# Hybrid decoder layer: weight-sum transfers re-placed, and the token operand of the sums made by ScalarE

## The chip, the cores and the metric

One core of a Trainium2 chip runs one launch of the whole layer. The metric is the time of that launch on the device in microseconds (us). TensorE is called PE, VectorE DVE, ScalarE ACT, GpSimd POOL and SyncE SP, as the profile names them.

## The reference

The layer works on 512 tokens of width 1024 in float32.

```python
h = x + 0.5 * swiglu(rmsnorm(x, norm_ffn1), ffn1_gate, ffn1_up, ffn1_down)      # d_ff = 2816
u = rmsnorm(h, norm_mix)
... = split(u @ w_in)            # q, k, v of two attentions, gates, merge gates ga and gb
o_a = nsa(...)                   # compressed + selected + window attention, 8 heads of 64
o_b = banded_attention(...)      # window 128, learned sinks, 8 heads of 64
merged = sigmoid(ga) * (o_a @ w_branch_a) + sigmoid(gb) * (o_b @ w_branch_b)
h = h + merged @ w_out
h = h + 0.5 * swiglu(rmsnorm(h, norm_ffn2), ffn2_gate, ffn2_up, ffn2_down)
out = rmsnorm(h, norm_final)
```

Only the last lines are touched: the merge, the product with w_out, and the second FFN (ffn2).

## The kernel before, in words

Every operand of a matmul is kept as two parts, a rounded high part and the rest (`split`, line 389: ACT copies the high part, DVE subtracts it). A product takes three matmuls: high by high, high by low, low by high. Activations lie with features on the partitions: `h`, `uh` and `ul` are 8 blocks of 128 features by 512 tokens.

**Weights.** `Weights` (line 67) streams the weights as blocks of 128 x 1024. SP loads a raw block (line 143), ACT writes the high part `whi` (line 151), DVE the low part `wlo` (line 155). The ring has four slots. `next()` hands out block p and first prepares block p + 2 (`AHEAD`), whose raw load went out earlier (four raw buffers). So the ACT and DVE work for block p + 2 stands in those engines' queues right in front of whatever the code emits after `next()` for block p. Each engine runs its instructions in the order in which the code emits them (`manual_schedule`, line 372), and waits on semaphores alone.

**Seven products for eight.** Four of the 22 column tiles of ffn2's gate and up (`FOURS`, line 34: 0, 8, 12 and 17, each 512 columns wide in effect) and two of its three down stages (`down`, line 1971) are done with seven block products in place of eight. This needs sums of weight quarters and sums of token quarters.

- The weight sums are made in DRAM by DMA alone. `four_steps` (line 414) gives eight transfers for a group, `down_sums` (line 403) eight for a down stage: copies from one DRAM tensor to another, or accumulating transfers. `issue` (line 397) puts them on POOL's queue (lines 399 and 401). A step that reads what an earlier one wrote waits for its landing. Three generators hand them out one at a time: `in_mixers` (line 421) for the groups of tiles 0 and 8 and the first down stage, during attention; `in_merge` (line 428) for the group of tile 12; `in_ffn2` (line 434) for the second down stage and then the group of tile 17, sixteen steps.
- The token sums are made by `sums_of_tokens` (line 1723) for `four_hi` and `four_lo`. A call with even f makes the first half for feature block k = f // 2: the token operand of the blocks k and 4 + k (line 1731: `uh + ul` on DVE), two differences (lines 1733, 1734) and their split. A call with odd f makes the second half (lines 1738, 1739, then 1740) from what the first left.

**The merge gates** (from line 1754). For each of eight blocks d: loads of stored gate pre-activations (`load_z`, line 1747, with a POOL product with the norm's rows, line 1750), a load of `h` (line 1755), for every other d a gate product, the two branch products with sigmoids, and the split of the merged block. At the end of each d one step of `in_merge` (line 1774). POOL therefore meets the steps between its products of line 1750.

**The w_out loop** (from line 1777). For each d: the product, the addition to `h` (line 1780), then `norm_in` (line 658): ACT makes `uh = h * gain` (line 661), DVE `ul` (line 662), ACT the square (line 672), POOL the running sum `sqacc` (line 673). From d = 4 on one call of `sums_of_tokens` follows.

**ffn2** (from line 2093). `TILES` (line 35) sets the order 4, 5, group 0, 6, 7, first down stage; group 8, group 12, 16, second down stage; group 17, 21, the rest. Amid tile 4's products the norm is made: column sums of `sqacc` by PE (`norm_col`, line 675), a power on POOL (line 686), a few small DVE operations, rows `r_b` by PE and ACT (`norm_rows`, line 695). Tiles 4 and 5 each end with the transposes of four blocks of `h` into `o_t` (`residual`, line 2009). In tile 5, `make_room` (line 1792) gives the room of `h` to `left`, the store of the down stage's operands; `gated` (line 1816) makes the gated product, and after each odd tile `operands` (line 1836) writes that store. Then come two calls of `sums_of_tokens` and one `next(steps)` (`steps` is `in_ffn2()`). `four` (line 1849) is a group: seven products of two blocks each, with `next(steps)` after two of them (line 1886); `down` calls `next(steps)` at four of its fourteen blocks (line 1983).

Of the kernel before, what the change touches and what calls it, by code (L numbers as in the profile page):

```python
# [11 lines left out]
AF = mybir.ActivationFunctionType  # L12
OP = mybir.AluOpType
# [49 lines left out]
def f32(ap):  # L63
    return ap.bitcast(F32)


class Weights:
# [112 lines left out]
    def next(self):  # L180
        i = self.pos
        self.prep(i + self.AHEAD)
        self.pos += 1
        return self.place(i)
# [178 lines left out]
def layer(ctx, tc, a, out):  # L363
# [641 lines left out]
    with ExitStack() as mixing:  # L1005
# [717 lines left out]
        def sums_of_tokens(f, p0, names):  # L1723


            k, second = f // 2, f % 2
            tt, stt = vector.tensor_tensor, vector.scalar_tensor_tensor
            if not second:
                x, y = tokens["a"] = [p0.tile([128, S], F32, name=names[0]) for _ in range(2)]
                for o, d in ((x, k), (y, 4 + k)):  # L1730
                    tt(o, f32(uh[:, d]), f32(ul[:, d]), op=OP.add)
                p = tokens["p"] = p0.tile([128, 2, 256], F32, name=names[1])
                tt(p[:, 0], y[:, 256:], x[:, 256:], op=OP.subtract)
                tt(p[:, 1], x[:, :256], x[:, 256:], op=OP.subtract)
            else:
                (x, y), s1 = tokens["a"], tokens["p"][:, 0]
                p = p0.tile([128, 2, 256], F32, name=names[1])
                stt(p[:, 0], s1, -1.0, x[:, :256], op0=OP.mult, op1=OP.subtract)
                stt(p[:, 1], y[:, :256], -1.0, p[:, 0], op0=OP.mult, op1=OP.subtract)
            split(four_hi[:, k, 2 * second:2 * second + 2], four_lo[:, k, 2 * second:2 * second + 2], p)  # L1740
# [3 lines left out]
        with pool("merge", 2, side="right") as mp:  # L1744
            mh, ml = (mp.tile([128, KD, S], F32R, name=n, bufs=1) for n in ("mh", "ml"))

            def load_z(d):
                z = mp.tile([128, S], F32, name="z%d" % (d // KD))
                nc.sync.dma_start(z, zd[d])
                gpsimd.tensor_tensor(z, z, r_b, op=OP.mult)  # L1750
                return z

            za, zb = load_z(0), None
            for d in range(KD):
                nc.sync.dma_start(h[:, d], hd[d])
                gates_z = [za, zb]
                if d + 1 < KD:
                    za = load_z(d + 1)
                if d not in GB_EARLY:
                    gates_z[1] = mp.tile([128, S], F32, name="z1")  # L1760
                    ps = acc(False)
                    mm3(ps, W.next(), u_in, KD)
                    vector.tensor_tensor(gates_z[1], ps, r_b, op=OP.mult)
                if d + 1 in GB_EARLY:
                    zb = load_z(KD + d + 1)
                for z, x in zip(gates_z[::-1], (b_in, a_in)):
                    scalar.activation(z, z, AF.Sigmoid)
                    ps = acc(False)
                    mm3(ps.rearrange("p (t c) -> p t c", t=4), W.next(), x, 4)
                    vector.tensor_tensor(z, z, ps, op=OP.mult)  # L1770
                y, z = gates_z
                vector.tensor_tensor(y, y, z, op=OP.add)
                split(mh[:, d], ml[:, d], y)
                next(merge_steps, None)

            m_in = (lambda k: mh[:, k]), (lambda k: ml[:, k])
            for d in range(KD):
                ps = acc(False)
                mm3(ps, W.next(), m_in, KD)
                vector.tensor_tensor(h[:, d], ps, h[:, d], op=OP.add)  # L1780
                norm_in(d, 2)
                if d > 3:
                    sums_of_tokens(d - 4, mp, ("z0", "z1"))


    with pool("temp3", 2) as temp, pool("end") as end:
# [184 lines left out]
        def down():  # L1971


            home = {1: "acc", 6: "acc", 7: "acc", 5: "o", 3: "o", 2: "s", 4: "s"}
            gets = {1: ((0, 0, 0.5),), 5: ((0, 1, 0.5), (1, 1, 0.5)), 2: ((0, 0, 0.5),), 6: (), 3: ((0, 1, -0.5),),
                    4: ((1, 0, 0.5),), 7: ()}
            more = {6: ((0, 1, OP.subtract),), 7: ((1, 0, OP.add), (1, 1, OP.subtract))}
            banks = {}
            u = [temp.tile([128, 512], F32, name="y") for _ in range(2)]
            for n, (m, g) in enumerate(STEPS):  # L1980
                if n == 0:
                    turn_back()
                if n % 3 == 2:
                    next(steps, None)
                if g == 0:
                    banks[m] = [psum.tile([128, 512], F32, name=home[m]) for _ in range(2)]
                wh, wl = (w.rearrange("p (a b) c -> p a (b c)", a=2) for w in W.next())
                for t in range(2):
                    ps, c = banks[m][t], slice(t * 128, t * 128 + 128)
                    for q in range(2):  # L1990
                        ah, al = (x[:, 2 * g + q, LEFT[m], c] for x in (left_hi, left["lo"]))
                        mm(ps, ah, wh[:, q], g == q == 0, False)
                        mm(ps, al, wh[:, q], False, False)
                        mm(ps, ah, wl[:, q], False, g == q == 1)
                    if g == 0:
                        continue
                    if m == 1:
                        scalar.activation(u[t], ps, AF.Identity, scale=0.5)
                    if m in more:
                        vector.scalar_tensor_tensor(u[t], ps, 0.5, u[t], op0=OP.mult, op1=OP.add)  # L2000
                    for i, k, by in gets[m]:
                        y = o_t[:, 2 * i + t, k * 512:k * 512 + 512]
                        vector.scalar_tensor_tensor(y, ps, by, y, op0=OP.mult, op1=OP.add)
                    for i, k, op in more.get(m, ()):
                        y = o_t[:, 2 * i + t, k * 512:k * 512 + 512]
                        vector.tensor_tensor(y, y, u[t], op=op)
            turn[0] = 0

        def residual(d):

            ps = tbank()
            for t in range(4):
                tensor.transpose(ps[:, t], h[:, d, t * 128:(t + 1) * 128], ident)
            scalar.copy(o_t[:, :, d * 128:(d + 1) * 128], ps)
# [78 lines left out]
        for third, tiles in enumerate(TILES):  # L2093
            if third == 2:
                make_room_again()
            for n, f in enumerate(tiles):
                if f in FOURS:
                    four(f - THIRDS[third][0], third < 2)
                    next(steps, None)
                    turn[0] = 2  # L2100
                    continue
                first = third == n == 0
                gate_at, up_at = {}, {}
                if n > 1 or third:
                    gate_at = {2: turn_back, 6: turn_back}
                    up_at = {2: turn_back, 6: lambda: back(3 - third)}
                z = []
                if third < 2:
                    up_at[4] = lambda: z.append(scaled(pg))
                pg = acc(False)  # L2110
                wp = W.next()
                settle(later)
                mm3(pg, wp, u_in, KD, col if first else gate_at)
                if third == 2:
                    back(2)
                    next(last)
                pu = acc(False)
                mm3(pu, W.next(), u_in, KD, rows if first else up_at)
                if third == 0 and n < 2:
                    for d in range(4 * n, 4 * n + 4):  # L2120
                        residual(d)
                if third == 0 and n == 1:
                    make_room()
                if third < 2 and n + 1 == len(tiles):
                    W.prep(W.pos + 2)
                if not z:
                    z.append(scaled(pg))
                gated(z[0], pu, f - THIRDS[min(third, 2) if f != 16 else 2][0], third == 0)
                if third == 0 and n < 2:
                    for i in (4 + 2 * n, 5 + 2 * n):  # L2130
                        sums_of_tokens(i, temp, ("y", "t"))
                if not first:
                    next(steps, None)
            if third < 2:
                down()
        for _ in last:
# [26 lines left out]
```

## Time and profile before

| | us |
|---|---|
| median of 3 runs | 1144.85 |
| lowest and highest | 1142.98 and 1148.29 |
| the profiled execution, its own time | 1142.28 |
| its span in the profile | 1140.5 |

Times in the profile are counted from the start of the span. In a row of the order of time, the first number is the start and the second the duration; the brackets hold the idle time of the engine before it and what ended that. `x2` marks rows that were merged. A row with SPq, or a DMA row of POOL, is the issue of a transfer, not the transfer. In a row that groups issues, the last number is the median from issue to landing. In the chain of waits a row is start, length and what the chain stood on. The gates run from about 632 to 714 us, the w_out loop to about 755, tiles 4 and 5 to about 792, the group of tile 0 to about 841, and the first down stage starts near 872.

### The profile page before, as it was taken

What the parts mean: (1) busy time and instruction counts of PE and PEld (TensorE: products, weight loads), DVE (VectorE), ACT (ScalarE), POOL (GpSimd) and SP (SyncE); (2) the same over time, 40 slices, a digit from 0 to 9 for tenths busy, and PEclk for the clock granted to TensorE, in tenths of its full rate; (3) what the DMA queues carried; (4) which work ended last, traced back from release to release, by engine and by line L of the source; (5) the groups of instructions that cost most, each with busy time, mean ns of one, the idle gap of its engine ahead of it and who ended that gap; (6) DMA issues with size and microseconds to landing.
All of it is one profiled execution on the core that took longest, in us unless ns stands there. A gap on an engine that the chain in (4) does not pass through costs nothing.

```text
span 1140.5 us, 15817 instructions
## 1 busy us (share of the span) xinstructions
PE 1095.8 (96%) x5827; PEld 937.1 (82%) x5827; DVE 767.1 (67%) x1366; ACT 536.5 (47%) x980; POOL 218.8 (19%) x253
## 2 busy tenths in 40 slices
PE   9999999999999998999999998979769999999987
PEld 7888899988888998998888886867657888888876
DVE  5656787844555588987777356575637876787663
ACT  5433344532334466767667333434324545454432
POOL 0312120000003145834345323111110000000002
PEclk9999999999999999999999999989889999999999
DMA  6988988787756265359997899619998555645611
GB/s 209 265 230 197 253 184 254 227 280 252 257 176 176 75 185 181 116 155 275 262 272 216 231 229 305 179 56 257 267 268 239 185 184 166 203 141 192 208 69 74
DMA packets 201413, 232.43 MB, mean 204 GB/s; under 512 B 7924, under 2 KB 152120, under 8 KB 201016
## 3 DMA queue, kind: packets, MB, share of 16 engines
q1 hardware_dynamic: 172696, 159.98, 44.2%
q0 software_dynamic: 26176, 67.11, 25.4%
q10 hardware_dynamic: 2464, 4.33, 1.0%
q8 instruction: 46, 0.75, 0.3%
q14 instruction: 31, 0.25, 0.1%
HBM read 211.47 MB, written 87.03 MB: 262 GB/s over the span
## 4 chain that ended last, share of the span: by engine, by line
PE 81%; DVE 8%; DMA 4%; ACT 3%; issue 2%; POOL 0%; SPq 0%; POOLq 0%; ACTq 0%; DVEq 0%
PE acc L387 25%; PE o L387 18%; PE s L387 17%; PE s L1880 4%; PE o L1880 3%; PE acc L1880 3%; PE o L791 3%; DMA raw<-in_ffn_gate_dram 3%; PE tp L1647 2%; PE s L791 2%; PE acc L791 2%; DVE wlo L155 2%; DMA z<-zd 1%; ACT whi L151 1%; PE tp L387 1%
## 5 line engine op out<-in xcount | busy, mean ns | idle before, releaser
L155 DVE TENSOR_TENSOR wlo<-raw,whi 128x1024 fp32r<-128x1024 f32 (+2 forms) x225 | 260.9, 1180 | 87.8 <-ACT whi L151 86.0
L151 ACT CAST whi<-raw 128x1024 fp32r<-128x1024 f32 (+2 forms) x250 | 228.8, 938 | 136.0 <-PE acc L387 24.7
L387 PE MATMUL acc<-uh,whi 128*128 128x512 f32 x224 | 91.9, 410 | 8.7 <-ACT whi L151 8.7
L387 PE MATMUL acc<-uh,wlo 128*128 128x512 f32 x224 | 88.9, 397 | 0.0
L387 PE MATMUL acc<-ul,whi 128*128 128x512 f32 x224 | 88.6, 395 | 0.0
L387 PE MATMUL acc<-whi,uh 128*128 128x256 f32 x224 | 65.9, 294 | 1.2 <-ACT whi L151 1.2
L387 PE MATMUL acc<-wlo,uh 128*128 128x256 f32 x224 | 63.6, 284 | 0.1
L387 PE MATMUL acc<-whi,ul 128*128 128x256 f32 x224 | 63.5, 284 | 0.0
L1662 DVE TENSOR_TENSOR pts<-tp,pts 128x512 fp32r<-128x512 f32 (+1 forms) x62 | 41.9, 686 | 22.1 <-ACT pts L1659 21.5
L387 PEld LDWEIGHTS acc<-uh,whi 128*128 128x128 f32 x224 | 42.9, 191 | 16.4 <-ACT whi L151 9.2
L2058 POOL TENSOR_TENSOR o_t<-o_t,g_b 128x512 f32<-128x512 f32 (+1 forms) x5 | 5.9, 1182 | 250.8 <-ACT z L2052 250.8
L387 PEld LDWEIGHTS acc<-uh,wlo 128*128 128x128 f32 x224 | 42.7, 190 | 10.7 <-DVE wlo L155 1.3
L1561 ACT ACTIVATE pbuf<-s,m 128x256 f32<-128x256 f32 (+3 forms) x96 | 47.5, 502 | 8.4 <-DVE c L1571 4.1
L387 PE MATMUL acc<-G,whi 128*128 128x512 f32 x164 | 50.5, 389 | 0.0
L387 PE MATMUL o<-G,whi 128*128 128x512 f32 x156 | 48.5, 391 | 1.0 <-ACT whi L151 0.5
L387 PE MATMUL s<-G,whi 128*128 128x512 f32 x160 | 49.4, 390 | 0.0
L387 PEld LDWEIGHTS acc<-ul,whi 128*128 128x128 f32 x224 | 42.9, 192 | 7.5
L387 PE MATMUL o<-uh,whi 128*128 128x512 f32 x120 | 48.0, 400 | 0.5 <-ACT whi L935 0.5
L1659 ACT CAST pts<-tp 128x512 fp32r<-128x512 f32 (+1 forms) x62 | 35.5, 585 | 24.9 <-PE tp L1647 19.1
L387 PE MATMUL o<-ul,whi 128*128 128x512 f32 x120 | 46.9, 390 | 0.0
L387 PE MATMUL o<-uh,wlo 128*128 128x512 f32 x120 | 46.8, 390 | 0.0
L1584 POOL TENSOR_SCALAR pbuf<-pbuf,c,gate 128x256 f32<-128x256 f32 (+3 forms) x57 | 35.0, 624 | 57.7 <-DVE c L1571 36.8
(471 smaller groups left out, 3030.8 us busy)
## 6 DMA issues: line engine op xcount, KB each, us to landing
raw<-in_ffn_gate_dram SPq DMA_DIRECT2D x42, 512.0 KB, 5.2
raw<-in_ffn_down_dram SPq DMA_DIRECT2D x34, 512.0 KB, 5.0
w<-in_ffn_up_dram POOLq DMA_DIRECT2D x16, 1024.0 KB, 11.5
raw<-w SPq DMA_DIRECT2D x32, 512.0 KB, 4.3
raw<-in_ffn_up_dram SPq DMA_DIRECT2D x30, 512.0 KB, 4.8
t<-in_ffn_down_dram POOLq DMA_DIRECT2D x12, 1024.0 KB, 10.5
raw<-in_w_in_dram SPq DMA_DIRECT2D x20, 512.0 KB, 6.1
raw<-s SPq DMA_DIRECT2D x16, 512.0 KB, 5.2
```

Of the source, the lines that this page charges most:

```text
L151: self.nc.scalar.copy(self.place(i)[0][:, k0:k1], self.raw[i][:, k0:k1])
L155: engine.tensor_tensor(lo, self.raw[i][:, k0:k1], f32(hi), op=OP.subtract)
L387: tensor.matmul(out, lhsT, rhs, start=start, stop=stop)
L791: tensor.matmul(o, a_[:, n], x(k), start=new and n == step == 0, stop=n == 7 and step == 2, skip_group_check=True)
L1561: scalar.activation(u.p[:, hd], b.view[:, j], AF.Exp, bias=u.m[:, hd:hd + 1], scale=-1.0, accum_out=u.sum[:, hd:hd + 1])
L1584: e.tensor_scalar(u.p[:, hd], u.p[:, hd], u.c[:, hd:hd + 1], u.gate[:, hd:hd + 1], op0=OP.mult, op1=OP.mult)
L1647: tensor.transpose(ps[:w, hd], u.p[:, hd, kb * w:kb * w + w], ident)
L1659: scalar.copy(p.hi, flat(b.ps)[:w])
L1662: vector.tensor_tensor(p.lo, flat(b.ps)[:w], f32(p.hi), op=OP.subtract)
L1880: tensor.matmul(ps, x, y[:, k], start=new and kk == k == step == 0, stop=kk == k == 1 and step == 2, skip_group_check=True)
L2058: gpsimd.tensor_tensor(y, y, left["g_b"][:, cs], op=OP.mult)
```

## The change

Five edits.

- In the merge gates a step of `in_merge` is issued only for even d; the other four go into the w_out loop, after `norm_in` and the sums of each odd d.
- The sums in the w_out loop: calls 0 and 1 at d = 4, 2 at d = 5, 3 at d = 6, none at d = 7.
- The token operand of a first half is made by ACT from `h` with the gain as its scale, where DVE added `uh` and `ul`.
- In ffn2, calls 4 to 7 of the sums stand before `make_room`, `scaled` and `gated` of their tile, where they stood after.
- `next(steps)`: at two blocks of a down stage (n = 4 and 11) in place of four, none after a group, one more after tile 4.

```diff
@@ sums_of_tokens, first half @@
                 for o, d in ((x, k), (y, 4 + k)):
-                    tt(o, f32(uh[:, d]), f32(ul[:, d]), op=OP.add)
+                    scalar.activation(o, h[:, d], AF.Identity, scale=gains[:, 2, d:d + 1])
@@ the merge gates @@
                 split(mh[:, d], ml[:, d], y)
-                next(merge_steps, None)
+                if d % 2 == 0:
+                    next(merge_steps, None)
@@ the w_out loop @@
                 norm_in(d, 2)
-                if d > 3:
-                    sums_of_tokens(d - 4, mp, ("z0", "z1"))
+                for i in {4: (0, 1), 5: (2,), 6: (3,)}.get(d, ()):
+                    sums_of_tokens(i, mp, ("z0", "z1"))
+                if d % 2:
+                    next(merge_steps, None)
@@ down @@
-                if n % 3 == 2:
+                if n in (4, 11):
                     next(steps, None)
@@ the loop over ffn2's tiles @@
                     four(f - THIRDS[third][0], third < 2)
-                    next(steps, None)
                     turn[0] = 2
                     continue
...
                         residual(d)
+                if third == 0 and n < 2:
+                    for i in (4 + 2 * n, 5 + 2 * n):
+                        sums_of_tokens(i, temp, ("y", "t"))
                 if third == 0 and n == 1:
                     make_room()
...
                 gated(z[0], pu, f - THIRDS[min(third, 2) if f != 16 else 2][0], third == 0)
-                if third == 0 and n < 2:
-                    for i in (4 + 2 * n, 5 + 2 * n):
-                        sums_of_tokens(i, temp, ("y", "t"))
-                if not first:
-                    next(steps, None)
+                next(steps, None)
```

## The prediction, made before the result was known

> **What bounds the kernel now.** I read the page first, for the engine that sets the time.
>
> ```profile
> span 1140.5 us, 15817 instructions
> PE 1095.8 (96%) x5827; PEld 937.1 (82%) x5827; DVE 767.1 (67%) x1366; ACT 536.5 (47%) x980; POOL 218.8 (19%) x253
> ```
>
> TensorE (PE) is busy 1095.8 of 1140.5 us. Work added to or removed from other engines is worth something only where PE stands still, so the question is where PE's idle time lies in the stretches that the diff touches. The table by stage gives that for the merge gates. Its columns are the stretch and its length, then busy time of PE, PEld, DVE, ACT and POOL, then the granted clock, the DMA share and GB/s.
>
> ```profile
> 632.00:714.00 82.00, 78.33 (x333) 62.42 (x332) 44.80 (x58) 30.69 (x50) 25.15 (x23) 0.98 0.94 259
> ```
>
> PE lacks 3.67 us in the gates (82.00 less 78.33), and the DMA share is 0.94 there. Next is PE's own order of time, from the gates through the w_out loop into the second FFN (ffn2), which shows the waits one by one.
>
> ```profile
> 685.94 0.73 PE L387 MATMUL o<-G,whi 128*128 128x512 f32 x2 [0.51 <-ACT whi L151]
> 691.62 0.79 PE L387 MATMUL s<-uh,whi 128*128 128x512 f32 x1 [2.39 <-ACT whi L151]
> 694.75 0.53 PE L387 MATMUL s<-uh,whi 128*128 128x512 f32 x1
> ...
> 738.39 0.39 PE L387 MATMUL acc<-mh,whi 128*128 128x512 f32 x1
> 743.60 0.39 PE L387 MATMUL acc<-mh,wlo 128*128 128x512 f32 x1
> ...
> 765.18 1.87 PE L387 MATMUL tp<-ones,sqacc 128*128 128x1 f32 x8 [6.23 <-POOL sqacc L673]
> ...
> 804.84 0.80 PE L1880 MATMUL s<-whi,fhi 128*128 128x512 f32 x1 [7.53 <-ACT whi L151]
> 810.53 0.63 PE L1880 MATMUL s<-whi,fhi 128*128 128x512 f32 x1
> ...
> 850.08 0.79 PE L387 MATMUL acc<-uh,whi 128*128 128x512 f32 x1 [8.73 <-ACT whi L151]
> ```
>
> Five waits, then. The normal step from matmul to matmul is (743.60 - 738.39) / 23 = 0.227 us (24 matmuls from the first row to the second, end to end). After the 2.39 us wait, six steps take 694.75 - 691.62 = 3.13 us, against 6 x 0.227 = 1.36: another 1.77 us lost to a slower clock. The clock column of the next table has 0.83 there.
>
> Last, what those waits hang on. POOL issues the weight-sum transfers (lines 399 and 401) between its own operations, and SP issues the loads.
>
> ```profile
> 668.91 1.06 POOL L399 DMA_DIRECT2D w<-in_ffn_up_dram  x1
> 673.45 1.02 POOL L399 DMA_DIRECT2D w<-in_ffn_up_dram  x1
> ...
> 769.88 1.54 POOL L401 DMA_DIRECT2D t<-in_ffn_down_dram  x2
> ...
> 867.72 1.01 POOL L399 DMA_DIRECT2D w<-in_ffn_gate_dram  x1 [5.74 <-DMA w<-w]
> 1109.75 1.29 POOL L2058 TENSOR_TENSOR o_t<-o_t,g_b 128x512 f32<-128x512 f32 x1 [241.02 <-ACT z L2052]
> ```
>
> ```profile
> 680.00:690.00 10.00, 8.71 (x36) 6.09 (x34) 4.65 (x6) 2.39 (x4) 2.60 (x3) 1.00 1.10 295
> 690.00:700.00 10.00, 8.34 (x29) 6.35 (x30) 7.31 (x9) 3.82 (x7) 3.02 (x3) 0.83 0.78 252
> ...
> 730.00:740.00 10.00, 10.00 (x46) 8.28 (x45) 5.25 (x5) 3.49 (x6) 2.43 (x2) 1.00 0.29 84
> ```
>
> ```profile
> 669.93 0.43 SPq L143 DMA_DIRECT2D raw<-in_w_branch_b_dram  x1
> ```
>
> ```profile
> 681.46 0.62 ACT L151 CAST whi<-raw 128x512 fp32r<-128x512 f32 x1 [2.83 <-DMA raw<-in_w_branch_b_dram]
> ```
>
> ```profile
> 677.65 10.98 DMA z<-zd
> ...
> 826.87 22.03 DMA raw<-in_ffn_gate_dram
> ```
>
> ```profile
> w<-in_ffn_up_dram POOLq DMA_DIRECT2D x8, 1024.0 KB, 12.3
> z<-zd SPq DMA_DIRECT2D x9, 256.0 KB, 5.2
> raw<-in_w_branch_b_dram SPq DMA_DIRECT2D x6, 256.0 KB, 5.6
> w<-w POOLq DMA_DIRECT2D x4, 6.3
> ```
>
> Two accumulating steps go out at 668.91 and 673.45; 12.3 us is the median landing of such a step. The DMA share is 1.10 from 680 to 690, full, and only 0.29 from 730 to 740: what is put off from the gates into the w_out loop finds room. In the full stretch a 256 KB weight load issued at 669.93 holds ScalarE until 681.46, 11.5 us against a median of 5.6, and a z load takes 10.98 against 5.2. ScalarE's weight copy is late, and PE waits 0.51 and 2.39 us for it.
>
> **The change, part by part.** (1) *Merge steps.* Of eight steps four stay with the gates (blocks 0, 2, 4, 6), four go into the w_out loop (blocks 1, 3, 5, 7). On POOL's queue the second step moves behind the z products of block 2, where now the third goes out at 668.91; the third moves to block 4, some 16 to 20 us later. So a plain copy goes at 668.91 and nothing at 673.45, and by the 6.3 us of a copy it is down by about 676. The late loads then arrive near their medians: the weight load at 676 to 678 in place of 681.46, z at 677.65 + 5.2 = 682.9 in place of 688.63. PE needs the block after the 2.39 us wait at about 688, and the sigmoid and the copy in front of it would be done by 686. So I take off 0.51 + 2.39 and the slow clock's 1.77: **-4.67 us**. Bounds: 0 if the loads stay late, 3.67 + 1.77 = -5.44 if the whole stage closes up.
>
> The Trainium skill (TensorE: Matmul & The Clock Gate, Part 1: The HAM clock gate) says that the clock falls after about 3.4 us of idling. By that rule a wait of 2.39 us costs no clock and this term would be -2.90. The row at 691.62 and the 0.83 speak the other way here, so the rows decide.
>
> The four moved steps meet other work in the w_out loop. On POOL they stand behind the squares of blocks 1, 3, 5 and 7. Two blocks are 24 x 2 x 0.227 = 10.9 us or more, against 6.3 us for a copy and 12.3 for an accumulation: only a late landing would hold up a square, and nobody needs the running sum before the last. The eighth step stands on POOL between the last square and the norm's power. Its issue takes 1.06 us as at 668.91, but after that square PE needs 1.87 us for the column sums (the row at 765.18), which hides it. If the seventh had not landed by then, everything from the power on would wait. Their traffic falls where the share was 0.29, and the weights are loaded four blocks ahead, 4 x 5.44 = 21.8 us: 0.
>
> (2) *Steps in groups and down stages.* POOL shows that they are not paced by their places. From 769.88 to 867.72 it does nothing but issue the sixteen steps, each held by a landing; its next operation is at 1109.75. Moving a step past matmuls, past DVE or ACT work, or to another tile leaves POOL's order as it is. This part doesn't do what it says: **0**. The eighth merge step now overlaps the first two of these; that is the rival on the other side below.
>
> (3) *The token operand.* Eight adds of two 128x512 tensors leave DVE, eight scaled ACT copies of the same size come.
>
> ```profile
> 738.59 0.69 DVE L1780 TENSOR_TENSOR h<-s,h 128x512 f32<-128x512 f32 x1 [0.94 <-PE s L387]
> 740.74 2.41 DVE L1731 TENSOR_TENSOR z<-uh,ul 128x512 f32<-128x512 f32 x2
> 746.72 0.68 DVE L1780 TENSOR_TENSOR h<-acc,h 128x512 f32<-128x512 f32 x1
> ...
> 761.76 0.68 DVE L1780 TENSOR_TENSOR h<-s,h 128x512 f32<-128x512 f32 x1
> ...
> 798.94 1.28 DVE L1731 TENSOR_TENSOR y<-uh,ul 128x512 f32<-128x512 f32 x2
> ```
>
> ```profile
> 739.31 0.72 ACT L661 ACTIVATE uh<-h,cols_c 128x512 fp32r<-128x512 f32 x1 [3.25 <-DVE h L1780]
> 739.94 0.62 ACT L672 ACTIVATE turn_a<-h 128x512 f32<-128x512 f32 x1
> 744.50 1.05 ACT L151 CAST whi<-raw 128x1024 fp32r<-128x1024 f32 x1
> ```
>
> In the w_out loop DVE paces the tail: from the h addition of block 4 to that of block 5 it takes 8.13 us, from there to block 7's 15.04, where PE's blocks take 24 x 0.227 = 5.44. The two adds take 2.41 us there, against 1.28 at 798.94, with a POOL square beside them. On ACT the two copies follow the square at steps of 739.94 - 739.31 = 0.63: starts at 740.57 and 741.20, the end 0.72 later at 741.92. DVE's differences start there, not at 740.74 + 2.41 = 743.15: -1.23 us for each first half. The second half now goes into the same block 4: DVE's low part (as an h addition, 0.69), two half-width differences (0.35 each) and ACT's copy (0.72) in front of the weight copy of 744.50, an estimated +2.11. Block 4 becomes 8.13 - 1.23 + 2.11 = 9.01, blocks 5 and 6, with one first and one second half as before, 15.04 - 1.23 = 13.81: 22.82 in place of 23.17, **-0.35**. It moves the last h addition (761.76), the last square and so the 6.23 us wait at 765.18, which ends with that square. Bounds +1.5 and -1.5: one more pass between ACT and DVE either way. If a weight copy behind the longer block 4 makes PE wait earlier, that only comes off the 6.23 us that PE waits anyway.
>
> (4) *Block 7's sums behind the norm.* With the last half moved into block 6, DVE is free for the norm about 2 us earlier. PE gets no use of it.
>
> ```profile
> 773.96 1.06 PE L387 MATMUL tp<-sqacc,ones 128*128 128x128 f32 x8
> ```
>
> ```profile
> 771.91 0.87 DVE L698 TENSOR_SCALAR sqacc<-ident,rcol 128x128 f32<-128x128 f32 x4
> ```
>
> After 765.18 PE has the column sums, two groups of the gate and six of the up product before it turns to the norm's rows at 773.96, and DVE had them at 771.91 + 0.87 = 772.78. **0**; bounds 0 to -0.5.
>
> (5) *Sums 4 to 7 ahead of the gated product.* The wait at 804.84 ends a relay of ACT and DVE that begins when ACT's last transposed copy is out.
>
> ```profile
> 791.37 1.08 ACT L2014 COPY o_t<-tp 128x512 f32<-128x512 f32 x2 [0.25 <-PE tp L2013]
> ...
> 803.75 1.99 ACT L151 CAST whi<-raw 128x1024 fp32r<-128x1024 f32 x2
> ```
>
> Between 791.37 + 1.08 = 792.45 and 803.75 stand the gated product with its operands and then sums 6 and 7. Their order is swapped; all of it stays between the same two ends, because the two new copies wait in ACT's order behind 791.37. Two adds (1.28) go, two copies come (0.72 + 0.63 = 1.35): **0**, bounds +1.5 and -1.5. The first writing of the operand store, in the room of h, must now wait for those copies; they end about 794, and the gated product that comes before that writing only begins behind them.
>
> Sum: -4.67 - 0.35 = **-5.0 us**. The profiled execution, 1142.28 us by its own time (span 1140.5 and 1.78 around it), would take 1137.3. It lies 2.57 below the median of three, 1144.85; against that median I forecast **1139.9 us**. What is won before the ffn2 chain starts moves the chain too, so it is kept.
>
> **Rivals.** *The loads stay late.* SP's queue and POOL's share the DMA engines. If what slows a load is that any POOL transfer is in flight, not how many, then a step at 668.91 harms the loads behind it as two did. For it: the gate load of 826.87 needs 22.03 us with one or two in flight. Against it: a single copy is down in 6.3 us, before z is asked for at 677.65. Only the 0.35 stays: 1144.5. The Trainium skill (DMA: Bandwidth & Descriptors, Queues, rings and completion order) says that each engine takes turns between its queues, packet by packet; that is this rival. The trace agrees for the 22.03 us load.
>
> *A wait in ffn2 gives way too.* At 804.84 PE waits 7.53 us and loses 810.53 - 804.84 - 12 x 0.227 = 2.97 more to the clock; at 850.08 it waits 8.73 for the 22.03 us load. Less DVE work or another meeting of steps and loads may halve one of them, some 5 us: 1134.9. Against it: the relay has the same length by (5), and the steps are still back to back.
>
> *The steps run into each other, slower.* The eighth merge step goes out near 765 and is in flight until about 777, under the first ffn2 steps. If that delays their whole chain by one landing, 12.3 us, the narrow gate and up loads of the next tile are starved as the first were, and PE meets a second wait like that of 850.08: 8.73 + 2.97 (clock, as at 804.84) = +11.7, less 5.0: 1151.6. It decides once the chain ends later than about 880, from 867.72 for its last issue. Against it: those loads come after, and 12.3 us is the whole step, while it only shares the engines.
>
> **How the numbers follow.** A measurement of this kernel can tell about 0.5%, 5.7 us, from no change. The forecast has 0.52; its own range is 1137 to 1143, since the merge term has its bounds and (3) and (5) each 1.5, and about a third of it lies beyond 5.7. Loads stay late 0.2 (no change to tell), a wait in ffn2 gives way 0.18 (faster), slower 0.1. Faster 0.52 / 3 + 0.18 = 0.35, slower 0.1 less some luck, 0.08, the same 0.57. The range, 1133.5 to 1145.5, takes in the first three cases and leaves the slower one out.
>
> **What would show it.** In the changed profile: POOL issues after 668.91 none until about 684 to 689; the DMA share of 680 to 690 under 0.9; no PE wait over 1 us in the gates and no slow clock there; four steps between the squares; the wait before the column sums still 5.5 to 6.5 us; some 7.5 us before the first group's second product; 8 to 9 us for the next tile's gate load; steps of ffn2 back to back for some 98 us. I am wrong if the gates still lack over 2.5 us of PE, if either ffn2 wait changes by over 3 us, or if the steps there wait for anything but landings.

## The result, and the profile after it

| | before | after |
|---|---|---|
| median of 5 runs, us | 1144.91 | 1137.67 |
| lowest and highest | 1142.98 and 1148.68 | 1136.13 and 1138.66 |
| the profiled execution, its own time | 1142.28 | 1138.66 |

The ratio after to before is 0.9926, its 95% interval 0.9903 to 0.995: the kernel is 7.2 us faster by the medians. The two profiled executions differ by 3.6 us only. Before's lies 2.6 us under its median and after's 1.0 over it, so the pair shows half of the gain. The stages below are compared in this pair, and the last microseconds of the difference are looked for at the end.

The first lines of the page of after:

```profile
span 1136.9 us, 15814 instructions
...
PE 1096.1 (96%) x5827; PEld 938.9 (83%) x5827; DVE 757.9 (67%) x1358; ACT 541.5 (48%) x988; POOL 218.8 (19%) x253
```

The table by stage of after, same columns as for before:

```profile
632.00:714.00 82.00, 82.00 (x365) 67.89 (x364) 48.36 (x63) 33.84 (x55) 23.16 (x20) 1.00 0.87 240
680.00:690.00 10.00, 10.00 (x46) 8.29 (x45) 7.56 (x11) 3.42 (x6) 2.94 (x3) 1.00 0.83 189
690.00:700.00 10.00, 10.00 (x46) 8.29 (x45) 5.66 (x9) 3.33 (x6) 4.34 (x4) 1.00 1.11 340
...
730.00:740.00 10.00, 10.00 (x46) 8.29 (x45) 5.53 (x10) 4.67 (x7) 2.04 (x2) 1.00 0.81 158
```

In the gates PE is busy for all of the 82 us, where it lacked 3.67, and the granted clock is 1.00. The traffic has gone where it was sent: 0.83 for 1.10 from 680 to 690, 0.81 for 0.29 from 730 to 740. From 690 to 700 the share is even higher than before, 1.11 for 0.78, and PE waits for nothing there. PE's order of time, every wait over 1 us from the gates to the down stage:

```profile
757.98 1.87 PE L387 MATMUL tp<-ones,sqacc 128*128 128x1 f32 x8 [5.84 <-POOL sqacc L673]
...
792.22 0.80 PE L1883 MATMUL acc<-whi,uh 128*128 128x512 f32 x1 [5.47 <-DVE t L1823]
...
838.68 0.80 PE L387 MATMUL acc<-uh,whi 128*128 128x512 f32 x1 [4.56 <-ACT whi L151]
...
851.62 2.33 PE L1919 MATMUL tp<-ident,t 128*128 128x128 f32 x8 [5.48 <-ACT G L1930]
```

The two waits of the gates are gone. The column sums still wait 5.84 us. The 7.53 us wait at the first group's second product is gone too, but a new one of 5.47 stands inside the first product, on a DVE operation (L1823). The gate of the next tile waits 4.56 in place of 8.73, and a second new wait, 5.48, follows at the group's transposes. POOL, with its issues of steps:

```profile
667.02 0.66 POOL L401 DMA_DIRECT2D w<-in_ffn_up_dram  x1
...
683.02 1.06 POOL L399 DMA_DIRECT2D w<-in_ffn_up_dram  x1
...
757.87 1.02 POOL L399 DMA_DIRECT2D w<-in_ffn_gate_dram  x1
760.14 1.04 POOL L686 TENSOR_TENSOR ny<-nv,mhalf 128x4 f32<-128x4 f32 x1 [1.25 <-DVE nv L684]
761.15 1.54 POOL L401 DMA_DIRECT2D t<-in_ffn_down_dram  x2
771.88 1.19 POOL L399 DMA_DIRECT2D t<-in_ffn_down_dram  x1 [9.19 <-DMA t<-in_ffn_down_dram]
...
862.35 1.02 POOL L399 DMA_DIRECT2D w<-in_ffn_gate_dram  x1 [5.19 <-DMA w<-w]
1106.28 1.29 POOL L2061 TENSOR_TENSOR o_t<-o_t,g_b 128x512 f32<-128x512 f32 x1 [242.92 <-ACT z L2055]
```

Nothing is issued between 667.02 and 683.02. Behind 761.15 POOL again does nothing but the sixteen steps, until 862.35.

To follow the gain I took the start of the same matmul in both traces and call before's less after's the lead. It is -0.2 us at the start of the gates and 5.9 at the start of w_out (710.24 and 704.38), 7.2 at the column sums (765.18 and 757.98), 6.4 at the norm's rows (773.96 and 767.52), 8.9 at the first group's third product, 11.4 at the next tile's gate (850.08 and 838.68). Then it falls: 5.2 at that tile's up product, 5.0 at the down stage, 3.6 at the end. So the gates win some 6 us, the w_out loop a little more, and in this pair ffn2 takes part of it back in two places.

### The profile page after: what moved, and what is told of

Its sections match the earlier page's. It is cut to its first block, busy times and chain, and to the rows that moved or that the text cites. A ratio compares the mean times of both kernels' runs of the same rounds, so it can differ in the third digit from the quotient of the medians.

```text
span 1136.9 us, 15814 instructions
## 1 busy us (share of the span) xinstructions
PE 1096.1 (96%) x5827; PEld 938.9 (83%) x5827; DVE 757.9 (67%) x1358; ACT 541.5 (48%) x988; POOL 218.8 (19%) x253
## 4 chain that ended last, share of the span: by engine, by line
PE 82%; DVE 8%; DMA 4%; ACT 3%; issue 2%; POOL 0%; POOLq 0%; ACTq 0%; DVEq 0%; SPq 0%
PE acc L387 27%; PE o L387 19%; PE s L387 18%; PE o L791 3%; PE o L1883 3%; PE acc L1883 2%; PE s L1883 2%; DMA raw<-in_ffn_up_dram 2%; PE tp L1647 2%; PE s L791 2%; PE acc L791 2%; DVE wlo L155 2%; ACT whi L151 1%; DMA raw<-in_ffn_gate_dram 1%; PE tp L387 1%
## 5 line engine op out<-in xcount | busy, mean ns | idle before, releaser
L387 PEld LDWEIGHTS acc<-uh,wlo 128*128 128x128 f32 x224 | 43.3, 193 | 10.7 <-DVE wlo L155 1.2
```

The lines of the kernel that those rows point to most:

```text
L387: tensor.matmul(out, lhsT, rhs, start=start, stop=stop)
```

## The experiments

Medians of this section stand beside runs of the kernel before on the same chip. For the first four those have a median of 1144.85 us.

**One part alone, and all but that part.** *Merge alone* is the kernel before with the merge edit; *all but merge* is the kernel after without it.

```diff
@@ merge alone, against before @@
-                next(merge_steps, None)
+                if d % 2 == 0:
+                    next(merge_steps, None)
...
                     sums_of_tokens(d - 4, mp, ("z0", "z1"))
+                if d % 2:
+                    next(merge_steps, None)
@@ all but merge, against after @@
-                if d % 2 == 0:
-                    next(merge_steps, None)
+                next(merge_steps, None)
...
-                if d % 2:
-                    next(merge_steps, None)
```

> The kernel before with the merge-step edit alone: four steps among the gates, four in the w_out loop; sums of tokens and all else as before. If the gain is that of the merge steps: 5.5 to 7 us less than before (ratio 0.994 to 0.995), PE idle in the gates (632 to 714 us) under 0.5 us, the wait before the column sums about 6.2 us, the wait before the first group's second product 7 to 8 us. If the gain is that of the token operand and the moved sums: within 2 us of before.

> The changed kernel with the merge steps as before, one for each of the eight gate blocks. If the gain is that of the merge steps: the gates lack 3 to 4 us of PE again with a slow clock behind the wait, and the time is within 3 us of before (ratio 0.997 to 1.000); what remains is 0.4 us of the w_out loop and the slow clock behind the wait in the first group, some 3 us less what the next load wait takes back. If the gain is that of the token operand and the moved sums: 5 to 7 us less than before.

Merge alone took 1135.96 us, ratio 0.9916 (0.9887 to 0.9945): 8.9 us by the medians where 5.5 to 7 were expected, but the interval takes in the 0.9926 of the whole change. All but merge took 1143.11, ratio 0.9991 (0.9966 to 1.0016). The gates of merge alone, then of all but merge with its longest wait there:

```profile
632.00:714.00 82.00, 82.00 (x364) 67.85 (x363) 48.74 (x63) 32.97 (x53) 21.57 (x18) 1.00 0.87 240
```

```profile
632.00:714.00 82.00, 77.92 (x325) 62.24 (x324) 43.05 (x56) 30.43 (x50) 23.65 (x23) 0.96 0.95 260
```

```profile
691.07 0.50 PE L387 MATMUL s<-uh,whi 128*128 128x512 f32 x1 [2.39 <-ACT whi L151]
```

The one edit carries the whole gain. From the start of the gates to that of w_out merge alone gains 6.1 us, as the kernel after does. Where the eight steps stay in the gates PE lacks 4.08 us there, and the 2.39 us wait is back.

**The places in ffn2 alone**, on the kernel before:

```diff
-                if n % 3 == 2:
+                if n in (4, 11):
                     next(steps, None)
...
                     four(f - THIRDS[third][0], third < 2)
-                    next(steps, None)
...
-                if not first:
-                    next(steps, None)
+                next(steps, None)
```

> The kernel before with the new places of the ffn2 steps alone. If POOL is not paced by places: ratio 1.000 within 0.002, all sixteen steps back to back for some 98 us from the norm's power on, the gate load of the next tile 20 to 22 us, and the profile tells how much two executions of the same order differ. If the places spread the steps: steps beyond 100 us, a shorter gate load, 3 to 9 us less.

1145.31 us, ratio 0.9993 (0.9968 to 1.0019). Every engine executes the same instructions in the same order as in the kernel before, but for the line numbers. This part of the change does nothing, as step (2) had it. The two executions also tell how much the steps of ffn2 differ from one to the next without any change: here the sixteen issues take 101.7 us, where those of before take 97.8 (769.88 to 867.72).

```profile
768.95 1.54 POOL L401 DMA_DIRECT2D t<-in_ffn_down_dram  x2
...
870.61 1.01 POOL L399 DMA_DIRECT2D w<-in_ffn_gate_dram  x1 [7.99 <-DMA w<-w]
```

**The sums of calls 4 to 7 put back.** The kernel after, with these calls behind the gated product again and their operand made by DVE:

```diff
+                    if names[0] == "y":
+                        tt(o, f32(uh[:, d]), f32(ul[:, d]), op=OP.add)
+                        continue
...
-                if third == 0 and n < 2:
-                    for i in (4 + 2 * n, 5 + 2 * n):
-                        sums_of_tokens(i, temp, ("y", "t"))
                 if third == 0 and n == 1:
...
                 gated(z[0], pu, f - THIRDS[min(third, 2) if f != 16 else 2][0], third == 0)
+                if third == 0 and n < 2:
+                    for i in (4 + 2 * n, 5 + 2 * n):
+                        sums_of_tokens(i, temp, ("y", "t"))
```

> The changed kernel with calls 4 to 7 of the sums as before: behind the gated product, operand by DVE. If swapping them only moves the wait of the first group from its second product to its first: one wait of 7 to 8 us in front of the second product with a slow clock behind it, the first product started at once; the second product itself then starts within 0.5 us of the changed kernel and the product behind it about 3 us later; in all 0 to 3 us more than the changed kernel, the more hidden the longer PE waits for the next loads anyway. If the swap is worth nothing: no difference in these rows. If it is most of the gain: 5 us more than the changed kernel.

1136.98 us, ratio 0.9928 (0.99 to 0.9956), as the kernel after. Its first group waits where before did:

```profile
797.24 0.79 PE L1886 MATMUL s<-whi,fhi 128*128 128x512 f32 x1 [7.53 <-ACT whi L151]
```

So the swap of step (5) moves the wait, from 7.53 us for the weights to 5.47 for a bank, and the time stays.

**How many steps must leave the gates?** Two kernels made from before: one in which block 3 hands out no step, so that the two accumulations of 668.91 and 673.45 no longer stand one block apart, the later steps come one block later, and the last of the eight lies in the w_out loop; and one in which all eight go into the w_out loop, one a block. Before, on the same chip, took 1144.03.

```diff
@@ one step moved @@
-                next(merge_steps, None)
+                if d != 3:
+                    next(merge_steps, None)
...
+                if d == 1:
+                    next(merge_steps, None)
@@ all in w_out @@
-                next(merge_steps, None)
...
                     sums_of_tokens(d - 4, mp, ("z0", "z1"))
+                next(merge_steps, None)
```

> The kernel before with one merge step less among the gates: none at block 3, the rest one block later, the last in the w_out loop at block 1. So only the second of the two accumulations that went out 4.5 us apart leaves its place. If it is that meeting of two which makes the loads late: the waits of 0.5 and 2.4 us in the gates and their slow clock go, 4 to 6 us less than before (ratio 0.995 to 0.9965). If it is the sum of the traffic in the gates, an eighth of which moves: under 1.5 us.

> The kernel before with all eight merge steps in the w_out loop, one for each block. If four steps fewer among the gates is all there is to gain: the gates at 82 of 82 us as with the merge steps alone, not better; but the steps then stand 5.4 to 8 us apart on POOL's queue while an accumulation takes 11 to 12 us, so POOL waits for landings in front of the squares, the last square comes 10 to 25 us late, and the norm with it: PE waits 15 to 30 us before the column sums, and the time is 5 to 20 us above before. If POOL's waits there cost nothing: the same time as with the merge steps alone, ratio 0.992.

One step moved took 1139.03 us, ratio 0.9959 (0.9937 to 0.9982); all in w_out 1136.58, ratio 0.9922 (0.9898 to 0.9945). The gates of the one, and of the other:

```profile
632.00:714.00 82.00, 80.75 (x353) 65.82 (x353) 46.54 (x62) 33.16 (x55) 24.51 (x23) 1.00 0.95 259
```

```profile
632.00:714.00 82.00, 82.00 (x363) 67.91 (x362) 47.28 (x63) 33.77 (x55) 20.84 (x17) 1.00 0.68 202
```

With one step moved the DMA share is 0.95 as before (0.94), and PE lacks 1.25 us for 3.67, all of it at the start of w_out. It starts w_out at 704.71, 5.53 us ahead of before; 0.67 of these it had at the start of the gates, so the gates give 4.9 of the 6.1 us that they give in the kernel after. So it is not the amount of traffic in the gates that costs, but where the steps lie in it: the pair of accumulations is parted. (The steps behind it have moved by a block too; that they have no share in the gain was not tried.) It gains less in the end, 5.0 us by the medians for the 7.5 of all in w_out. The difference is there by the first products of w_out (at before's 712.07), where counted from the start of the gates one step moved leads before by 4.9 us, and the kernel after, merge alone and all in w_out by 7.0. All in w_out gains as much as moving half of the steps. Its last two steps do hold POOL up, and it costs nothing:

```profile
754.39 0.53 POOL L401 DMA_DIRECT2D w<-w  x1 [4.68 <-DMA w<-in_ffn_up_dram]
756.54 1.26 POOL L673 TENSOR_TENSOR sqacc<-sqacc,turn_a 128x512 f32<-128x512 f32 x1 [1.62 <-ACT turn_a L672]
761.05 1.03 POOL L399 DMA_DIRECT2D w<-in_ffn_gate_dram  x1 [3.25 <-DMA w<-w]
```

```profile
757.86 1.87 PE L387 MATMUL tp<-ones,sqacc 128*128 128x1 f32 x8 [6.24 <-POOL sqacc L673]
```

POOL waits 4.68 us for a landing, then still 1.62 for ACT's square: the landing came first. The last step holds POOL 3.25 us ahead of the norm's power, when PE already has the column sums. The column sums wait 6.24, as in before. Late squares, which an expectation above reckons with, did not come; the steps of the w_out loop land faster than I had taken from the gates.

**Does the bank or the weights hold the first group?** Two kernels from after. Both multiply tile 5's second factor out of its PSUM bank before the sums of calls 6 and 7. *Weights early* also splits a weight block of the group there (the line `W.prep`); *bank only* is without that line. The sums use another buffer name, so that they don't wait for the factor.

```diff
+                t = None
+                if third == 0 and n == 1:
+                    t = temp.tile([128, S], F32, name="t")
+                    vector.tensor_tensor(t, pu, r_b, op=OP.mult)
+                    W.prep(W.pos + 3)
...
-                        sums_of_tokens(i, temp, ("y", "t"))
+                        sums_of_tokens(i, temp, ("y", "s" if n else "t"))
```

> The changed kernel with, in tile 5, the second factor of the gated product and the weight copies of the first group's second product emitted ahead of sums 6 and 7. If the wait in the first group is the place of these copies in the queues of ACT and DVE: it goes (5.5 us and its slow clock, about 3), the second product starts 6 us earlier; then the narrow gate and up loads of the next tile, 17 to 22 us each beside the steps, take half or more of it back: 2 to 6 us less than the changed kernel. If the first group waits for the sums themselves: the wait stays, no difference.

> The kernel after, with the second factor of tile 5 multiplied on VectorE ahead of the sums of calls 6 and 7 and nothing else: the weights are split where they were. The PSUM bank that the first product of the down stage waits for is read some 5 us earlier. Theory (the wait only changes place between bank and weights): the 5.47-us wait at the first product goes, a wait of 5 to 7.5 us for the weights (ScalarE's whi) stands at the second product instead, as in the kernel before, and the time is that of the kernel after within 1 us, 1137 to 1138. Rival (the bank was what cost, the weights come early enough since the sums now lie behind the multiplication): no wait over 1.5 us at either product, and 1132 us, as with the early weights.

(Where the second of these speaks of the first product of the down stage, the first group's is meant.)

Weights early took 1131.98 us, ratio 0.989 (0.9855 to 0.9924), 4.6 us less than all in w_out on the same chip. Bank only, run later beside a before of 1145.6, took 1136.7, ratio 0.9914 (0.9899 to 0.9929). The wait of bank only in the first group, and that of weights early:

```profile
798.27 0.80 PE L1884 MATMUL s<-whi,fhi 128*128 128x512 f32 x1 [6.67 <-ACT whi L151]
```

```profile
801.39 0.80 PE L1884 MATMUL o<-whi,fhi 128*128 128x512 f32 x1 [4.19 <-ACT whi L151]
```

The bank alone is worth nothing that shows: its wait goes, and 6.67 us of waiting for weights take its place. The rival in the expectation for bank only, 1132, has fallen. With the weights early there is no wait at either of these products; 4.19 us come at the third.

**What takes the gain back in ffn2?** In after, steps are issued back to back, and the narrow weight loads beside them, those of a tile's gate and up in pieces of 128 columns or 512 bytes, are slow. *Steps held* makes their places count. Before each step but the second, which follows the first at once, POOL multiplies one column that ACT has just copied, so POOL cannot issue it before ACT has reached that place. Two steps lie in tile 4, one in tile 5, one in the first group, four in the first down stage, eight later.

```diff
+        marks = end.tile([128, 2, 17], F32, name="marks")
+        marked = [0]
+        def held():
+            i = marked[0]
+            marked[0] += 1
+            m = marks[:, :, i:i + 1]
+            scalar.copy(m[:, 0], ones[:, :1])
+            gpsimd.tensor_tensor(m[:, 1], m[:, 0], m[:, 0], op=OP.mult)
+            next(steps, None)
@@ four @@
-                if m in (5, 7):
-                    next(steps, None)
+                if m == 5 or m == 7 and marked[0] > 4:
+                    held()
@@ down @@
-                if n in (4, 11):
-                    next(steps, None)
+                if n % 3 == 2:
+                    held()
@@ the loop over ffn2's tiles @@
-                next(steps, None)
+                if third == 0 and n < 2:
+                    held()
+                if first:
+                    next(steps, None)
```

*Held and early* has this and the weights early.

> The changed kernel with POOL really held: in front of each ffn2 step POOL reads one column that ACT wrote in its order at that place; places: two steps in tile 4, one in tile 5, one in the first group, four in the first down stage, then two in each group and four in the second down stage; none beside the loads of the tiles that follow the first group. If the transfers in flight make the narrow loads late: the gate load of the next tile takes 5 to 8 us, not 17 to 22, the waits of 4.6 and 5.5 us behind the first group go, 6 to 11 us less than the changed kernel. If the loads are late for another reason, or the second group's loads then wait for the sums: no gain, or more time.

> The edits of the two kernels before this one together: VectorE is held up less in tile 5, and GpSimd is really held back, so that few DRAM-to-DRAM steps run beside the weight loads behind the last square. Theory (two separate prices): the 5.47-us wait at the first product of the first down stage and the load waits behind it were paid one after the other, so the gains add. The wait of 5.47 goes, none over 1.5 us stands between the row sums and the second down stage but for the column sums' 5.8, and the time is 1127.25 less 5.3, about 1122 us (1120 to 1124). Rival A (the early weights only pull the next wait forward): a wait of about 4.2 us at the second product, as with the early weights alone, and 1126 us. Rival B (the gains were the same microseconds twice): no gain over the held steps, 1127 us.

(The second of these, too, means the first group where it speaks of the first product of the down stage.) Steps held took 1127.25 us, ratio 0.9855 (0.9822 to 0.9888). Held and early took 1123.5, ratio 0.9814 (0.9797 to 0.9831), the fastest kernel of this study. POOL's steps around the first group in steps held:

```profile
800.82 1.18 POOL L399 DMA_DIRECT2D t<-in_ffn_down_dram  x1 [0.45 <-issue]
864.56 0.87 POOL L1978 TENSOR_TENSOR marks<-marks 128x1 f32<-128x1 f32 x1 [62.55 <-ACT marks L1977]
865.37 0.54 POOL L401 DMA_DIRECT2D t<-t  x1
```

Between the two POOL waits 62.55 us for ACT's mark. The stretch from 765 to 870 in after, in steps held and in held and early:

```profile
765.00:870.00 105.00, 86.62 (x374) 68.84 (x373) 56.88 (x77) 45.67 (x61) 12.24 (x14) 0.92 0.97 261
```

```profile
765.00:870.00 105.00, 96.13 (x433) 76.68 (x432) 66.40 (x91) 52.95 (x75) 6.85 (x9) 0.98 0.55 166
```

```profile
765.00:870.00 105.00, 98.89 (x452) 80.43 (x451) 70.06 (x95) 54.83 (x76) 9.10 (x11) 0.98 0.59 179
```

The DMA share falls from 0.97 to 0.55, and PE does 9.5 us more work in the same 105 us. The load of the next tile's gate, in the DMA issues from 820 to 821 of after, then of steps held:

```profile
raw<-in_ffn_gate_dram SPq DMA_DIRECT2D x1, 512.0 KB, 17.2
```

```profile
raw<-in_ffn_gate_dram SPq DMA_DIRECT2D x1, 512.0 KB, 4.9
```

17.2 us have become 4.9. Behind the first group's first product no wait over 0.6 us is left before the down stage. Later, between 870 and 1060, PE does lack 4.3 us in steps held against 0.3 in after, where the steps now run. Of held and early only the time came as the theory said (1122, within 1120 to 1124). It has a wait of 4.28 us at the third product, the one that rival A expected at the second, and one of 2.83 at the transposes of a later group. In ratios the early weights are worth 0.004, 4.7 us, on top of the held steps, where 5.3 were expected; the two intervals overlap a little.

## Why the prediction came out as it did

The forecast was 1139.9 us, 5.0 less than before; the median is 1137.67, 7.2 less and inside the range. Its main step, (1), holds; step (5) does not stand as written, and the sentence on the chain does not hold in the profiled pair. That the number came close is in part luck: the gates and the w_out loop give 7.4 us in the pair (from a lead of -0.2 to one of 7.2), and ffn2 and the clock of the tail take 3.6 of them back. Neither the larger gain nor what is taken back was in the sum.

*(1) Merge steps: right in mechanism, too small.* -4.67 was put down, and the gates give 5.9 + 0.2 = 6.1 us by the pair. The sum counted the two waits of the gates and six slow steps. It left out what goes with each: 0.28 beside the first (two blocks apart the lead grows by 0.79, the wait is 0.51), 0.57 beside the second (5.68 us from 685.94 to 691.62, where 12 matmuls of 0.227 and the wait of 2.39 make 5.11), 0.17 more of slow clock, and 0.36 at the first product of w_out. With these 1.38 it is 6.05. In the w_out loop the 0.53 us wait of before at 711.5 and its slow clock went as well, another 0.95. The upper bound, -5.44, was thus no bound: it took PE's idle time up to 714 and a clock loss from one place.

The reason given, a single copy in the place of the two accumulations, fits the trace of after: the copy issued at 667.02 lands in 5.3 us, and ACT splits the block for which it stood until 681.46 before without a wait for its load.

```profile
678.64 0.60 ACT L151 CAST whi<-raw 128x512 fp32r<-128x512 f32 x1
```

One step moved, which leaves the share of DMA as it is, points to the pair: there a single accumulation goes out at 668.14, the next at 683.80, and 4.9 of the 6.1 us are there. The rival "the loads stay late" is out for the gates. In ffn2, where a step follows every landing, loads do stay late.

*The four moved steps: 0, right.* Four lie between the squares, and the column sums wait 5.84 us. All in w_out shows how much room there was.

*(2) The places in ffn2 do nothing: right*, by the identical instructions and 0.9993.

*(3) The token operand: -0.35 forecast, -0.40 measured.* The rows of the first sums in after:

```profile
731.78 0.69 DVE L1781 TENSOR_TENSOR h<-s,h 128x512 f32<-128x512 f32 x1 [0.95 <-PE s L387]
...
735.01 0.46 DVE L1733 TENSOR_TENSOR z<-z,z 128x256 f32<-128x256 f32 x1 [1.00 <-ACT z L1731]
...
740.83 0.68 DVE L1781 TENSOR_TENSOR h<-acc,h 128x512 f32<-128x512 f32 x1
...
754.55 0.68 DVE L1781 TENSOR_TENSOR h<-s,h 128x512 f32<-128x512 f32 x1
```

```profile
733.66 1.32 ACT L1731 ACTIVATE z<-h,cols_c 128x512 f32<-128x512 f32 x2
```

From block 4's addition to block 5's it takes 9.05 us (9.01 forecast), from there to block 7's 13.72 (13.81). DVE's first difference starts as ACT's two copies end.

*(4) Block 7's sums behind the norm: 0.* The norm's rows are ready at 763.18 + 0.87 = 764.05, long before PE turns to them at 767.52; no use of it, as said.

```profile
763.18 0.87 DVE L698 TENSOR_SCALAR sqacc<-ident,rcol 128x128 f32<-128x128 f32 x4
```

*(5) Sums ahead of the gated product: 0 in the sum, wrong in the mechanism.* The step swapped two parts of a relay "between the same two ends". It looked at ScalarE's split of the weights alone. The gated product's first operation is also what empties the PSUM bank (the place of a matmul's results) of tile 5's up product, and the first group needs that bank for its second half of tokens. Behind the two new copies and the sums it comes late:

```profile
785.90 1.33 ACT L1731 ACTIVATE y<-h,cols_c 128x512 f32<-128x512 f32 x2
```

```profile
787.26 0.43 DVE L1733 TENSOR_TENSOR t<-y 128x256 f32<-128x256 f32 x1 [3.64 <-ACT y L1731]
...
791.48 0.68 DVE L1823 TENSOR_TENSOR t<-acc,r_b 128x512 f32<-128x512 f32 x1
```

PE reaches that bank at 786.75 (792.22 less 5.47) and gets it when the multiplication of 791.48 is done. It cost nothing in the sum because under it the weights of the next product were split: 0.32 us is left there of 7.53. "Some 7.5 us before the first group's second product" in what would show it is therefore wrong, and by the text's own test, a change of over 3 us in either wait of ffn2, its account of ffn2 fails, at this wait and at the gate's (4.56 us in place of 8 to 9). The other signs came as listed, but for POOL's issue at 683.02, a microsecond early, and a chain of 101 us instead of 98. Bank only shows that the two waits lie behind one another: either one is paid in any order.

*"What is won before the ffn2 chain starts moves the chain too, so it is kept": only partly in this pair.* The chain of steps starts 8.7 us earlier (761.15 for 769.88), but its last issue is 5.4 earlier (862.35 for 867.72): it takes 101.2 us for 97.8. The eighth merge step, out at 757.87, is in flight below the first two, and the third goes out 10.7 us behind them, for 8.1 in before. That is the place which the rival on the other side named, with 12.3 us. But the longer chain cannot be put down to it: with that step in flight the chain takes 97.6 us in merge alone and 98.9 in bank only, and without it 101.7 in the kernel with the ffn2 places alone. What makes a chain longer stays open. PE cannot run away from the chain: two weight loads meet it, the gate's at 838.68 and then the up's. The chain of waits of after has the second:

```profile
824.09 20.19 DMA raw<-in_ffn_up_dram
```

That load takes 20.19 us, ScalarE's queue stands behind it, and the transposes wait 5.48. The lead falls from 11.4 to 5.2 there, about the lead of the chain itself. Steps held shows it: with the chain out of the way the load waits go, and with them 8 us by the ratios (0.9926 less 0.9855), 10 by the medians. How much ffn2 takes back in the median is not shown: the pair ends 3.6 us apart, while the medians differ by 7.2, which is the whole lead at the column sums.

*The last 1.4 us* of the pair's difference are clock. In the group of tile 17 PE waits some 2.8 us for DVE in every one of these kernels. After, then before:

```profile
1083.68 0.33 PE L1919 MATMUL tp<-ident,t 128*128 128x128 f32 x1 [2.83 <-DVE t L1869]
...
1085.53 0.63 PE L387 MATMUL acc<-ul,whi 128*128 128x512 f32 x1
1085.95 0.63 PE L387 MATMUL acc<-uh,wlo 128*128 128x512 f32 x1
```

```profile
1088.72 0.33 PE L1916 MATMUL tp<-ident,t 128*128 128x128 f32 x1 [2.83 <-DVE t L1866]
...
1090.25 0.40 PE L387 MATMUL acc<-uh,whi 128*128 128x512 f32 x1
1090.48 0.39 PE L387 MATMUL acc<-ul,whi 128*128 128x512 f32 x1
```

In after seven matmuls behind it take steps of 0.43 us, in before none. The twelve profiled executions have none in four (before, all but merge, the ffn2 places, one step moved) and seven to ten in eight.

## What to carry to other kernels

Before spreading transfers thinner, look for the two that are in flight together where a load is late: moving one of them by a block brought 4.9 of the 6.1 us in the gates here, and 5.0 of 7.5 in the whole kernel. On a queue where each step already waits for a landing, a step's place in the program did nothing (0.9993); if it must not start yet, give it something to wait for. When work is put ahead of an operation, ask which PSUM bank or buffer that operation sets free, as well as which engine it keeps busy.

## What the runs showed of the hardware

The next tile's gate load, 512 KB in narrow pieces, takes 4.9 us with no DRAM-to-DRAM step beside it (steps held), 17.2 beside them in after and 22.03 in before. Where two steps are issued together in ffn2, the third goes out 8.1 us behind them in before, and 10.7 in after with an earlier one still in flight.

Whether a wait costs clock depends on more than its length. The 2.39 us wait of the gates was followed by slow matmuls in before; the 2.83 us wait of the tail in eight of twelve executions. The column sums' wait of 5.84 to 6.23 us is followed by slow matmuls each time, but by 7 in before, 9 with the sums put back, 11 in after and 14 in merge alone, some 0.2 us each. The Trainium skill (TensorE: Matmul & The Clock Gate, Part 1: The HAM clock gate) says that the clock is decided over free-running windows of about 3.4 us, which do not start anew with the kernel. That fits counts which vary with the phase; a wait shorter than the window that slows the clock does not follow from its rule of a whole idle window, and the measured rows stand against that.
